# Order of the queries' and shares' pieces, and of the norm's reciprocals, in a hybrid attention layer on one core

## The chip, the core and the metric

The kernel runs on one core of a Trainium2 chip. Time is device microseconds (us) of that core; the time before is the median of three runs. The core has five engines with a stream of instructions each: TensorE (PE, matmuls; PEld are its weight loads), VectorE (DVE), ScalarE (ACT), GpSimd (POOL) and SyncE (SP), which issues most of the transfers (DMAs). Each engine takes its instructions strictly in order, and they wait for one another by semaphores.

## The reference

One layer of an encoder with two attention mixers side by side, over 512 tokens and 16 meta tokens of width 2048. Mixer A has 8 query heads on 2 key heads of 128, with normalised queries and keys and a rotary embedding; mixer B has 8 heads of differential attention: two score maps on halves of 64 columns, the second softmax taken off the first with a factor. Both are gated, joined, projected and normalised.

```python
hn = rmsnorm(h, pre_norm_g[layer])
proj = jnp.einsum('bld,dc->blc', hn, w_in[layer])
qa, ka, va, ga, qb, kb, vb, gb = jnp.split(proj, SPLIT_POINTS, axis=-1)
...
    # mixer A
    s = jnp.einsum('bkgqd,bksd->bkgqs', qs[0], k).astype(jnp.float32) * scale
    p = jax.nn.softmax(s, axis=-1)
    return jnp.einsum('bkgqs,bksd->bkgqd', p.astype(v.dtype), v)
...
    # mixer B
    s1 = jnp.einsum('bhqd,bhkd->bhqk', qs[0], k1).astype(jnp.float32) * scale + bias
    s2 = jnp.einsum('bhqd,bhkd->bhqk', qs[1], k2).astype(jnp.float32) * scale + bias
    a = jax.nn.softmax(s1, axis=-1) - lam * jax.nn.softmax(s2, axis=-1)
    return jnp.einsum('bhqk,bhkd->bhqd', a.astype(v.dtype), v)
...
y = jnp.einsum('blc,cd->bld', jnp.concatenate([ya, yb], axis=-1), w_out[layer])
h = h + rmsnorm(y, post_norm_g[layer])
```

## The kernel before

**Two pieces of each number.** Matmuls run on a rounded type (`fp32r`). Every operand is therefore split into a high piece, rounded by a copy on ACT (`hi`, L349), and a low piece, the rest, by a subtraction on DVE (`lo`, L352); a product takes three matmuls (high·high, low·high, high·low). Weights arrive as `st` and are split into `wh` (ACT, L156) and `wl` (DVE, L157); the list `splits` keeps these instructions, so that others can be put behind them.

**Projections and heads.** The program runs one dense projection after the other (`dense_T`, tile `pd` in PSUM, four banks): for each head of mixer B the gate, values, keys and queries of the next head; then queries, keys and values of mixer A; then mixer A's eight gates; at the end the output product `po`. Between these matmuls PE runs the attention of heads that have begun: scores `sc`, sums of squares `ss`, transpositions `tr` and the products of shares and values `pv`. The class `Lanes` decides the order on PE while the program is written: it keeps a clock of planned matmul time, and each head is a generator that yields the lag (table `LAG`, in us) after which its next matmuls may stand. PE's instructions and the weights' loads keep their program order. The order on the other engines is made by a scheduler from the program, its priorities and its dependences; `tc.issue_after(i)` adds the condition that an instruction stands behind `i`.

**Mixer B.** `queries_B` scales the projection into `qf` (DVE) and makes two maps: `q1`, `q2` (high) and `l1`, `l2` (low), each in two halves of 64 partitions, as keys are stored high and low on the two halves (`s1`, `s2` of `keys_B`). `attention_B` takes four tiles of 128 queries. For each map it computes `sc`, then DVE's reduction L533 puts the bias on, writes `p` and finds the bound `mx`; ACT's exponential (L541) follows, DVE's reciprocal, POOL's normalisation of map 1 (L546), DVE's combination (L548) and two transposes (L460, L462) into `pt`. There is one bank pair for `sc`, so each map's scores wait for the reduction of the last. After two tiles `regroup` sends `pt` to DRAM (`turn`) and back as `pl` by transfers on SP; `p_times_v` splits that into `ph` (ACT) and `pl` (DVE), with `pm` for the meta tokens, and multiplies by the values (`pv`). `finish_B` norms a finished head: squares, `ss` on PE, ACT's square root, four reciprocals of 128 columns (L578, each behind the newest reduction), two multiplications on DVE, and a store of `gB` to `oscr`. `finish_head(h - 1)` is where the program makes sure that this has been written.

**Sums of output weights.** `weigh()` is called five times per head: it issues the load of a block of weights into a scratch tile `ws` on SP, and, one step later, a transfer on POOL's queue that accumulates another block on it (L821).

**Mixer A.** `attention_A` transposes queries, splits them into `qh` and `qlA`, and runs the same steps with one map (reduction L636 to `mxA`, exponential L639, POOL L641). Beside it `silu_A` takes a gate's projection out of PSUM (`gt`, DVE L597) and through ACT's SiLU (L598), and `gate_A` multiplies it on the head's `oA`. ACT loads a table whenever it goes from exponentials to SiLU or back. `half_dead` splits the output of mixer B for the output product (`ah`, `al`, `bh`, `bl`).

## Time and profile before

| | |
|---|---|
| median of three runs | 899.06 us (898.26 to 902.3) |
| the profiled execution, its own time | 901.28 us |
| its span, first to last instruction | 899.5 us |
| mean granted TensorE clock | 0.997 |
| transfers | 185.49 MB, mean 206 GB/s |
| mixer B, 0 to 480 us: PE busy | 469.54 us |
| mixer A, 480 to 743.9 us: PE busy | 253.85 us |
| output product, 743.9 to 899.5 us: PE busy | 146.91 us |

In the profile `L533` is line 533 of the kernel before. A line with a helper (`hi`, `lo`, `mm`) stands for all its callers, so the tile names tell which is meant. A row of a timeline has the start, the duration, engine, line, operation, what it writes and reads, and in brackets the idle time of its engine before it and what ended that. PE's matmuls are pipelined: they start some 0.12 us apart with 264 columns although each is shown as 0.28.

### The profile page before, as it was taken

Reading aid. Unit: us, or ns where it says so; the run is one execution under the profiler, and the core shown is the slowest. Engines: PE = TensorE matmul, PEld = TensorE weight load, DVE = VectorE, ACT = ScalarE, POOL = GpSimd, SP = SyncE. Lnnn points to the kernel's source line nnn. Section 1 sums busy time; section 2 is a strip of 40 time slices with the busy share of each in tenths; the row PEclk is TensorE's granted clock in tenths of the full one; section 3 lists DMA queues with packets and bytes.
Section 4 is the critical chain, followed back from the end, with each engine's and each line's share of the span. In section 5 each row is a group of like instructions: output and inputs, shape, how many; then the busy total and the mean of one; then the engine's idle time right before and its main releaser. Section 6 shows DMA issues by size and latency. Waiting matters only on the chain. (4 is left out here: it accounts for less than half of the span.)

```text
span 899.5 us, 14066 instructions
## 1 busy us (share of the span) xinstructions
PE 870.3 (97%) x5130; PEld 769.9 (86%) x5130; DVE 631.4 (70%) x1137; ACT 497.9 (55%) x844; POOL 124.9 (14%) x168
## 2 busy tenths in 40 slices
PE   9999999999999999999999999999999989999996
PEld 8999898998989889888898888987878778888884
DVE  6577786857857568485683485788666675886886
ACT  6565564637546474464654444656566555665561
POOL 0100220211011121101120021342111210000010
PEclk9999999999999999999999999999999999999998
DMA  9754979887696877868553334456566658989883
GB/s 336 262 163 144 236 216 258 201 233 194 198 260 155 247 212 222 241 170 238 143 181 94 105 94 149 144 168 182 170 181 217 181 167 283 317 275 308 272 276 152
DMA packets 80677, 185.49 MB, mean 206 GB/s; under 512 B 15136, under 2 KB 38560, under 8 KB 80224
## 3 DMA queue, kind: packets, MB, share of 16 engines
q1 hardware_dynamic: 75856, 167.81, 57.1%
q0 software_dynamic: 4608, 16.78, 11.3%
q8 instruction: 40, 0.66, 0.3%
q14 instruction: 29, 0.24, 0.1%
q10 hardware_dynamic: 144, 0.01, 0.0%
HBM read 158.34 MB, written 59.77 MB: 242 GB/s over the span
## 5 line engine op out<-in xcount | busy, mean ns | idle before, releaser
L61 PE MATMUL pd<-xh,wh 128*128 128x264 f32 (+1 forms) x992 | 325.8, 328 | 0.0
L61 PE MATMUL pd<-xl,wh 128*128 128x264 f32 (+1 forms) x992 | 323.1, 326 | 0.0
L61 PE MATMUL pd<-xh,wl 128*128 128x264 f32 (+1 forms) x992 | 322.7, 325 | 0.4 <-DVE wl L157 0.4
L156 ACT ACTIVATE wh<-st 128x1024 fp32r<-128x1024 f32 (+2 forms) x159 | 165.5, 1041 | 187.1 <-PE pd L61 92.4
L157 DVE TENSOR_TENSOR wl<-st,wh 128x1024 fp32r<-128x1024 f32 (+2 forms) x159 | 191.1, 1202 | 86.6 <-ACT wh L156 86.2
L61 PEld LDWEIGHTS pd<-xh,wl 128*128 128x128 f32 x992 | 186.5, 188 | 16.5 <-DVE wl L157 0.8
L61 PEld LDWEIGHTS pd<-xh,wh 128*128 128x128 f32 x992 | 186.8, 188 | 12.3 <-ACT wh L156 0.2
L61 PEld LDWEIGHTS pd<-xl,wh 128*128 128x128 f32 x992 | 187.0, 189 | 10.6
L541 ACT ACTIVATE p<-p,mx 128x528 f32<-128x528 f32 x64 | 47.1, 736 | 58.8 <-DVE mx L533 58.6
L61 PE MATMUL pd<-wh,xh 128*128 128x512 f32 x128 | 50.4, 394 | 0.0
L460 DVE STREAM_TRANSPOSE pt<-p 128x512 f32<-128x512 f32 x64 | 45.0, 702 | 7.1 <-POOL p L641 6.4
L61 PE MATMUL pd<-wh,xl 128*128 128x512 f32 x128 | 49.9, 390 | 0.0
L61 PE MATMUL pd<-wl,xh 128*128 128x512 f32 x128 | 49.9, 390 | 0.0
L639 ACT ACTIVATE p<-p,mxA 128x528 f32<-128x528 f32 x32 | 23.6, 737 | 46.2 <-DVE mxA L636 46.1
L533 DVE CUSTOM_DVE_ANT_0 p<-sc,dist 128x528 f32<-128x528 f32 x64 | 43.9, 686 | 4.7 <-PE sc L61 4.3
L821 POOL DMA_DIRECT2D ws<-in_w_o_dram x32 | 26.7, 834 | 146.0 <-DMA ws<-ws 64.0
L546 POOL TENSOR_SCALAR p<-p,sm 128x528 f32<-128x528 f32 x32 | 22.8, 711 | 173.2 <-DVE sm L543 164.9
L641 POOL TENSOR_SCALAR p<-p,smA 128x528 f32<-128x528 f32 x32 | 26.4, 826 | 119.1 <-DVE smA L640 97.9
L352 DVE TENSOR_TENSOR pl<-pl,ph 128x1024 fp32r<-128x1024 f32 x32 | 39.2, 1226 | 3.2 <-ACT ph L349 2.3
L61 PE MATMUL pv<-pl,vh 128*128 128x256 f32 x128 | 36.6, 286 | 4.4 <-DVE pl L352 4.4
L61 PE MATMUL sc<-s,q 128*128 128x264 f32 x128 | 35.3, 295 | 3.9 <-DVE mx L533 3.9
L548 DVE SCALAR_TENSOR_TENSOR p<-p,c 128x528 f32<-128x528 f32 x32 | 24.5, 766 | 20.7 <-POOL p L546 20.5
(223 smaller groups left out, 1569.8 us busy)
## 6 DMA issues: line engine op xcount, KB each, us to landing
st<-in_w_t_dram SPq DMA_DIRECT2D x82, 512.0 KB, 5.1
turn<-pt SPq DMA_DIRECT2D x32, 544.0 KB, 3.0
pl<-turn SPq DMA_DIRECT2D x128, 128.0 KB, 3.9
ws<-in_w_o_dram POOLq DMA_DIRECT2D x32, 512.0 KB, 8.1
st<-ws SPq DMA_DIRECT2D x32, 512.0 KB, 4.4
st<-in_w_o_dram SPq DMA_DIRECT2D x22, 512.0 KB, 4.3
ws<-in_w_o_dram SPq DMA_DIRECT2D x16, 512.0 KB, 6.7
ws<-ws SPq DMA_DIRECT2D x16, 512.0 KB, 7.0
```

The costliest lines, as they stand in the source:

```text
L61: self._add(self.nc.tensor.matmul(out, lhsT, rhs, start=start, stop=stop, **kw), us)
L156: splits.append((nc.scalar.activation(wh[:, c], st[:, c], AF.Copy), nc.vector.tensor_tensor(out=wl[:, c], in0=st[:, c], in1=wh[:, c].bitca ...
L157: nc.vector.tensor_tensor(out=wl[:, c], in0=st[:, c], in1=wh[:, c].bitcast(F32), op=ALU.subtract)))
L352: nc.vector.tensor_tensor(out=dst, in0=src, in1=h.bitcast(F32), op=ALU.subtract)
L460: nc.vector.transpose(pt[:, :1024].rearrange("p (m c t q) -> p c m t q", m=4, c=TT, t=2)[:, :, :, j], p[:, NM:].rearrange("p (c m q) -> p ...
L533: maxima.append(nc.vector.tensor_tensor_reduce(out=two(p), in0=sc[:, :, :HALF], in1=two(dist[:, w0:w0 + NT]), scale=-0.125 / slope(h), sca ...
L541: nc.scalar.activation(p2[m], p2[m], AF.Exp, scale=-1.0, bias=mx[:, m:m + 1], accum_out=sm[:, m:m + 1])
L546: nc.gpsimd.tensor_scalar(out=p2[0], in0=p2[0], scalar1=sm[:, 0:1], scalar2=1.0, op0=ALU.mult, op1=ALU.mult)
L548: nc.vector.scalar_tensor_tensor(out=p2[0], in0=p2[1], scalar=c2, in1=p2[0], op0=ALU.mult, op1=ALU.add)
L639: nc.scalar.activation(p, p, AF.Exp, scale=-1.0, bias=mx, accum_out=sm)
L641: nc.gpsimd.tensor_scalar(out=p, in0=p, scalar1=sm, scalar2=1.0, op0=ALU.mult, op1=ALU.mult)
L821: nc.gpsimd.dma_start(out=dst, in_=src, accum_op=ALU.add)
```

## The change

It changes orders and no arithmetic.

- `queries_B` and `keys_B` write their pieces map by map: both high pieces of map 1, its two low ones, then map 2.
- `q_last` holds the newest queries' last high and last low piece, and `p_last` the shares' `pm` and `pl`; `behind_all` puts instructions behind these. In `p_times_v`, `ph` and `pm` stand behind the queries' last high piece, `pl` behind their last low one.
- Gates (`silu_A`) and the splits of `half_dead` stand behind the newest `pm` and `pl`; exponentials of mixer A behind the newest `pm`.
- `finish_B` yields after each of the first three reciprocals, where it yielded after the second alone, so that each next one goes behind a later reduction.
- `finish_head(h - 1)` is called after the keys' projection; in its old place the program only makes sure that the head's scores and last product are written (`products_B`).

```diff
--- before.py
+++ after.py
@@ -346,10 +346,10 @@
     L, U = slice(0, 64), slice(64, 128)
 
     def hi(dst, src):
-        nc.scalar.activation(dst, src, AF.Copy)
+        return nc.scalar.activation(dst, src, AF.Copy)
 
     def lo(dst, src, h):
-        nc.vector.tensor_tensor(out=dst, in0=src, in1=h.bitcast(F32), op=ALU.subtract)
+        return nc.vector.tensor_tensor(out=dst, in0=src, in1=h.bitcast(F32), op=ALU.subtract)
 
     def keys_B(pss, after=nullcontext):
         kf = ap.tile([P, NT], F32, name="kf", tag="tT")
@@ -357,10 +357,9 @@
         s1 = ap.tile([P, NT], F32R, name="s1", tag="s1")
         s2 = ap.tile([P, NT], F32R, name="s2", tag="s2")
         with after():
-            hi(s1[L], kf[L])
-            hi(s2[U], kf[U])
-            lo(s1[U], kf[L], s1[L])
-            lo(s2[L], kf[U], s2[U])
+            for s, a, b in ((s1, L, U), (s2, U, L)):
+                hi(s[a], kf[a])
+                lo(s[b], kf[a], s[a])
         return s1, s2
 
 
@@ -383,6 +382,17 @@
 
     def slope(h):
         return 2.0 ** (h - 2)
+
+
+    q_last, p_last = [None, None], [None, None]
+
+    @contextmanager
+    def behind_all(*ins):
+        with ExitStack() as stack:
+            for i in ins:
+                if i is not None:
+                    stack.enter_context(tc.issue_after(i))
+            yield
 
     def queries_B(h, pss, after=nullcontext):
         qf = ap.tile([P, NT], F32, name="qf", tag="tT")
@@ -395,14 +405,12 @@
         l2 = ap.tile([P, SEQ], F32R, name="l2", tag="ql", bufs=4)
         to, qf = [dealt(t) for t in (q1, l1, q2, l2)], by_token(qf)
         with after():
-            hi(to[0][L], qf[L])
-            hi(to[2][U], qf[U])
-            hi(to[0][U], qf[L])
-            hi(to[2][L], qf[U])
-            lo(to[1][L], qf[L], to[0][L])
-            lo(to[3][U], qf[U], to[2][U])
-            lo(to[1][U], qf[L], to[0][L])
-            lo(to[3][L], qf[U], to[2][U])
+
+            for q, l, a, b in (to[:2] + [L, U], to[2:] + [U, L]):
+                hi(q[a], qf[a])
+                q_last[0] = hi(q[b], qf[a]).ins
+                lo(l[a], qf[a], q[a])
+                q_last[1] = lo(l[b], qf[a], q[a]).ins
         return (q1, l1), (q2, l2)
 
     def values(pss, lag=LAG["vals"]):
@@ -483,10 +491,11 @@
         pm = ap.tile([96, 2 * P], F32R, name="pm", tag="pm", bufs=1)
         pt = pl.bitcast(F32)
 
-        with tc.issue_after(splits[-1][0].ins):
+        with behind_all(splits[-1][0].ins, q_last[0]):
             hi(ph, pt)
-            hi(pm[0:32], pf)
-        lo(pl, pt, ph)
+            p_last[0] = hi(pm[0:32], pf).ins
+        with behind_all(q_last[1]):
+            p_last[1] = lo(pl, pt, ph).ins
         nc.gpsimd.tensor_scalar(out=pm[32:64], in0=pm[0:32].bitcast(F32), scalar1=1.0,
                                 scalar2=1.0, op0=ALU.mult, op1=ALU.mult)
         lo(pm[64:96], pf, pm[0:32])
@@ -555,6 +564,7 @@
                             LAG["pB"])
             if half == 0:
                 yield LAG["scB"]
+        products_B[h] = last
         over[h] = lanes.spawn(finish_B(h, o), LAG["fin"], last)
 
     def finish_B(h, o):
@@ -576,7 +586,7 @@
 
             with tc.issue_after(maxima[-1].ins):
                 nc.vector.reciprocal(out=sq[:, tq], in_=sq[:, tq])
-            if t == 1:
+            if t < TT - 1:
                 yield LAG["scB"]
         nc.vector.tensor_tensor(out=o, in0=o, in1=sq, op=ALU.mult)
         nc.vector.scalar_tensor_tensor(out=gB[h], in0=o, scalar=sgc, in1=gB[h],
@@ -594,8 +604,9 @@
 
     def silu_A(pss):
         g = gp.tile([P, SEQ], F32, name="gt", tag="gt")
-        nc.vector.tensor_tensor(out=g, in0=pss[0], in1=rB[:, NM:], op=ALU.mult)
-        nc.scalar.activation(g, g, AF.Silu)
+        with behind_all(*p_last):
+            nc.vector.tensor_tensor(out=g, in0=pss[0], in1=rB[:, NM:], op=ALU.mult)
+            nc.scalar.activation(g, g, AF.Silu)
         return g
 
     def gate_A(h, g):
@@ -614,8 +625,8 @@
         tr = ptr.tile([P, 512], F32, name="tr", tag="tr")
         for t in range(TT):
             transpose(tr[:, t * P:(t + 1) * P], qn[t][:, h % 4, :], ident)
-        hi(dealt(qh), by_token(tr))
-        lo(dealt(ql), by_token(tr), dealt(qh))
+        q_last[0] = hi(dealt(qh), by_token(tr)).ins
+        q_last[1] = lo(dealt(ql), by_token(tr), dealt(qh)).ins
         yield LAG["qA"]
         while not k_task[3]:
             yield 0.3
@@ -636,7 +647,8 @@
                 maxima.append(nc.vector.tensor_tensor_reduce(
                     out=two(p), in0=sc[:, :, :HALF], in1=two(zed[0][:, :NT]), scale=-ASCALE,
                     scalar=3.0e38, op0=ALU.add, op1=ALU.min, accum_out=mx))
-                nc.scalar.activation(p, p, AF.Exp, scale=-1.0, bias=mx, accum_out=sm)
+                with behind_all(p_last[0]):
+                    nc.scalar.activation(p, p, AF.Exp, scale=-1.0, bias=mx, accum_out=sm)
                 nc.vector.reciprocal(out=sm, in_=sm)
                 nc.gpsimd.tensor_scalar(out=p, in0=p, scalar1=sm, scalar2=1.0,
                                         op0=ALU.mult, op1=ALU.mult)
@@ -872,7 +884,7 @@
     v = values(pss)
     with behind():
         gB = [gate(first[2], "gB0")] + [None] * (NH - 1)
-    heads, over = [None] * (2 * NH), [None] * (2 * NH)
+    heads, over, products_B = [None] * (2 * NH), [None] * (2 * NH), [None] * NH
 
     def finish_head(h):
         lanes.finish(heads[h])
@@ -890,11 +902,14 @@
             pss = dense_T(KEYS)
             if h:
                 weigh()
-                finish_head(h - 1)
+
+                lanes.finish(heads[h - 1])
+                lanes.finish(products_B[h - 1])
             v = values(pss)
             ks = keys_B(dense_T(KEYS))
             if h:
                 weigh()
+                finish_head(h - 1)
             qs = queries_B(h + 1, dense_T(REAL))
     weigh()
     def start_heads(grp, qn, q_task, k, v):
@@ -957,7 +972,8 @@
                     with tc.issue_after(splits[-4][1].ins):
                         TTv(out=sd, in0=st, in1=sd, op=SUB)
                     st = sd
-                split(to[i], st)
+                with behind_all(*p_last):
+                    split(to[i], st)
 
     for h in range(NH):
         if h == 5:
```

**DVE, head 4's queries.** These are DVE's instructions around the queries of mixer B's head 4. Rows name line, operation, output, inputs and shape; line numbers of the change are its own, so L542 is the reduction that was L533. Before:

```order
L390 SCALAR_TENSOR_TENSOR qf_2948<-pd_2865,rB_537 128x512
L157 TENSOR_TENSOR wl_2966<-st_2870,wh_2965 128x1024
L352 TENSOR_TENSOR pl_2761<-pl_2761,ph_2983 128x1024
L352 TENSOR_TENSOR l1_2952<-qf_2948,q1_2950 64x4x4x32
L352 TENSOR_TENSOR l2_2953<-qf_2948,q2_2951 64x4x4x32
L352 TENSOR_TENSOR l1_2952<-qf_2948,q1_2950 64x4x4x32
L352 TENSOR_TENSOR l2_2953<-qf_2948,q2_2951 64x4x4x32
L352 TENSOR_TENSOR pm_2984<-pt_2614,pm_2984 32x256
L533 ISA p_3005,mx_2998<-sc_3000,dist_558 128x528
```

and with the change:

```order
L400 SCALAR_TENSOR_TENSOR qf_2948<-pd_2872,rB_537 128x512
L157 TENSOR_TENSOR wl_2966<-st_2877,wh_2965 128x1024
L352 TENSOR_TENSOR l1_2952<-qf_2948,q1_2950 64x4x4x32 x2
L352 TENSOR_TENSOR l2_2953<-qf_2948,q2_2951 64x4x4x32 x2
L352 TENSOR_TENSOR pl_2749<-pl_2749,ph_2977 128x1024
L352 TENSOR_TENSOR pm_2978<-pt_2595,pm_2978 32x256
L542 ISA p_3005,mx_2998<-sc_3000,dist_558 128x528
```

The low part `pl` of the shares moved from in front of the four `l` to behind them, and the two pieces of `l1` now stand together in front of those of `l2`.

**DVE, the reciprocals of head 3's norm**, during the scores of head 4 (L533, in the change L542, is a score reduction; L578, in the change L588, a reciprocal). Before:

```order
L533 ISA p_3187,mx_3180<-sc_3182,dist_558 128x528
L533 ISA mx_3180 128x1
L460 STREAM_TRANSPOSE pt_2997<-p_3086 128x4x4x32
L462 STREAM_TRANSPOSE pt_2997<-p_3086 128x32
L578 RECIPROCAL sq_3073<-sq_3073 128x128 x4
L533 ISA p_3229,mx_3180<-sc_3224,dist_558 128x528
L533 ISA mx_3180 128x1
L581 TENSOR_TENSOR oB_2419<-oB_2419,sq_3073 128x512
L157 TENSOR_TENSOR wl_3193<-st_3017,wh_3192 128x1024
L582 SCALAR_TENSOR_TENSOR gB3_2514<-oB_2419,sgc_551,gB3_2514 128x512
L543 RECIPROCAL sm_3181<-sm_3181 128x2
L533 ISA p_3271,mx_3264<-sc_3266,dist_558 128x528
```

and with the change:

```order
L542 ISA p_3180,mx_3173<-sc_3175,dist_558 128x528
L542 ISA mx_3173 128x1
L468 STREAM_TRANSPOSE pt_2997<-p_3083 128x4x4x32
L470 STREAM_TRANSPOSE pt_2997<-p_3083 128x32
L588 RECIPROCAL sq_3070<-sq_3070 128x128 x2
L542 ISA p_3218,mx_3173<-sc_3213,dist_558 128x528
L542 ISA mx_3173 128x1
L588 RECIPROCAL sq_3070<-sq_3070 128x128
L157 TENSOR_TENSOR wl_3192<-st_3017,wh_3191 128x1024
L552 RECIPROCAL sm_3174<-sm_3174 128x2
L554 TENSOR_TENSOR c2_3223<-sm_3174,nlam_557 128x1
L542 ISA p_3261,mx_3254<-sc_3256,dist_558 128x528
```

Of the four in a row two are left in front of the reduction `mx_3180` (now `mx_3173`), one stands behind it, and the fourth follows behind the next reduction, further on. The multiplications L581 and L582 come later still.

**DVE, around the queries `qlA_7274` of mixer A** (L597, in the change L608, takes a gate out of PSUM; L460 and L462, in the change L468 and L470, are transposes of shares). Before:

```order
L157 TENSOR_TENSOR wl_7265<-st_7105,wh_7264 128x1024
L352 TENSOR_TENSOR pl_7032<-pl_7032,ph_7218 128x1024
L352 TENSOR_TENSOR pm_7219<-pt_6958,pm_7219 32x256
L640 RECIPROCAL smA_7235<-smA_7235 128x1
L352 TENSOR_TENSOR qlA_7274<-tr_7275,qh_7273 128x4x4x32
L460 STREAM_TRANSPOSE pt_7184<-p_7194 128x4x4x32
L462 STREAM_TRANSPOSE pt_7184<-p_7194 128x32
```

and with the change:

```order
L157 TENSOR_TENSOR wl_7265<-st_7105,wh_7264 128x1024
L352 TENSOR_TENSOR pl_7032<-pl_7032,ph_7218 128x1024
L352 TENSOR_TENSOR pm_7219<-pt_6958,pm_7219 32x256
L652 RECIPROCAL smA_7235<-smA_7235 128x1
L608 TENSOR_TENSOR gt_7258<-pd_6931,rB_537 128x512
L468 STREAM_TRANSPOSE pt_7184<-p_7194 128x4x4x32
L470 STREAM_TRANSPOSE pt_7184<-p_7194 128x32
L468 STREAM_TRANSPOSE pt_7184<-p_7243 128x4x4x32
L470 STREAM_TRANSPOSE pt_7184<-p_7243 128x32
L352 TENSOR_TENSOR qlA_7274<-tr_7275,qh_7273 128x4x4x32
```

The gate product `gt_7258`, which stood further ahead, and both pairs of transposes moved in front of `qlA_7274`.

**POOL, mixer B's head 4** (L821, in the change L833, is the accumulating transfer; L546, in the change L555, the normalisation of a tile's shares). Before:

```order
L490 TENSOR_SCALAR pm_2984<-pm_2984 32x256
L821 DMA ws100_580<-in_w_o_dram 128x1024
L821 DMA ws101_581<-in_w_o_dram 128x1024
L546 TENSOR_SCALAR p_3005<-p_3005,sm_2999 128x528
L546 TENSOR_SCALAR p_3086<-p_3086,sm_3080 128x528
L546 TENSOR_SCALAR p_3187<-p_3187,sm_3181 128x528
L546 TENSOR_SCALAR p_3271<-p_3271,sm_3265 128x528
L821 DMA ws102_582<-in_w_o_dram 128x1024
```

and with the change:

```order
L499 TENSOR_SCALAR pm_2978<-pm_2978 32x256
L833 DMA ws100_580<-in_w_o_dram 128x1024
L833 DMA ws101_581<-in_w_o_dram 128x1024
L555 TENSOR_SCALAR p_3005<-p_3005,sm_2999 128x528
L555 TENSOR_SCALAR p_3083<-p_3083,sm_3077 128x528
L833 DMA ws102_582<-in_w_o_dram 128x1024
L555 TENSOR_SCALAR p_3180<-p_3180,sm_3174 128x528
L555 TENSOR_SCALAR p_3261<-p_3261,sm_3255 128x528
```

The two transfers ahead of the first normalisation keep their place, and the transfer to `ws102` moved from behind the fourth to between the second and the third.

## The prediction

> **What bounds the kernel now.** I read the page's busy shares first, then the chain that ended last, then the list of what TensorE (PE) waits for, then timelines around those waits.
>
> ```profile
> PE 870.3 (97%) x5130; PEld 769.9 (86%) x5130; DVE 631.4 (70%) x1137; ACT 497.9 (55%) x844; POOL 124.9 (14%) x168
> PE po L61 16%; PE pd L61 1%; PE pv L61 1%; DVE y L1151 0%; DMA pt<-turn 0%; ACT jko L1066 0%; DVE y L1069 0%; DVE y L1157 0%; DVE pl L352 0%; DVEq L1259 0%; ACT bh L349 0%; DVE bl L352 0%; DVE ssy L1162 0%; ACTq L1066 0%
> ```
>
> PE is busy for 97% of the span; the change leaves its 5130 matmuls as they are. The last 16% of the span, the output product `po`, is one chain on PE, where the change touches nothing. So the time can change only by what PE waits in the attention before it.
>
> ```profile
> PE sc L61 <- DVE l L352: 4.7, 4, 1.2
> PE pv L61 <- DVE pl L352: 4.4, 4, 1.5
> PE sc L61 <- DVE mx L533: 3.9, 7, 0.9
> PE sc L61 <- DVE qlA L352: 2.1, 4, 1.1
> PE sc L61 <- ACT qh L349: 1.1, 1, 1.1
> PE pv L61 <- ACT ph L349: 0.9, 2, 0.5
> ```
>
> This is the list of PE's waits, grouped by what ended them: us in total, times, the longest. These six rows add to 17.1 us, 1.9% of the span: that is nearly all there is to win. Against it stand the waits that the change makes itself. A difference of 0.5%, 4.5 us, is about what a measurement of this kernel can tell from no change.
>
> **Part 1, the share's low part behind the queries' (mixer B).** In head 4 VectorE (DVE) makes the low part `pl` of the last head's shares, then the four low parts `l` of the new queries:
>
> ```profile
> 258.57 1.22 DVE L352 TENSOR_TENSOR pl<-pl,ph 128x1024 fp32r<-128x1024 f32 x1
> 259.71 2.88 DVE L352 TENSOR_TENSOR l<-qf,q 64x512 fp32r<-64x512 f32 x4
> 261.84 0.39 PE L61 MATMUL sc<-s,l 128*128 128x264 f32 x1 [1.17 <-DVE l L352]
> 262.07 0.28 PE L61 MATMUL sc<-s,q 128*128 128x264 f32 x1
> ```
>
> The first score product waits 1.17 us for map 1's second piece, the third of the four. The change takes `pl` (1.22 us) from in front, and makes map 1's second piece the second, 0.7 us (2.88/4) sooner. Head 3 shows the new order already, since there the scheduler had put `pl` last:
>
> ```profile
> 204.20 2.81 DVE L352 TENSOR_TENSOR l<-qf,q 64x512 fp32r<-64x512 f32 x4
> 206.34 0.39 PE L61 MATMUL sc<-s,l 128*128 128x264 f32 x1
> 207.03 1.23 DVE L352 TENSOR_TENSOR pl<-pl,ph 128x1024 fp32r<-128x1024 f32 x1
> ```
>
> There no wait is listed; only the matmul's 0.39 in place of 0.28 tells that it came out of a short stop. I leave 0.2 us in each of heads 4 to 7: 4.7 − 4 × 0.2 = **−3.9 us**. What then comes late is `pl` itself, by the `l`s' 2.9 us; no `pv` of mixer B has a row that waits on it now (all four are in mixer A). If that cover is gone, it costs at most 2.9 us a head.
>
> **Part 2, one reciprocal per score.** In head 4 the four reciprocals of head 3's norm stand as a block in front of a score reduction `mx`:
>
> ```profile
> 282.03 3.34 DVE L578 RECIPROCAL sq<-sq 128x128 f32<-128x128 f32 x4
> 286.00 0.39 PE L61 MATMUL sc<-s,q 128*128 128x264 f32 x1 [0.68 <-DVE mx L533]
> ...
> 384.27 0.39 PE L61 MATMUL sc<-s,q 128*128 128x264 f32 x1 [0.29 <-DVE mx L533]
> 392.60 0.39 PE L61 MATMUL sc<-s,q 128*128 128x264 f32 x1 [0.43 <-DVE mx L533]
> ```
>
> With two in front and one behind each of the next reductions, `mx` starts 1.7 us earlier and the wait of 0.68 goes. Of the seven waits on `mx` five stand behind such reciprocals; I keep the two others, 0.29 and 0.43 in head 6: 3.9 − 0.7 = **−3.2 us**. The finish of a head (two multiplications on DVE, the store of `gB` on SP's queue) comes later, but nobody reads it before the output. On SP a load of the weights' sums, `ws`, moves in front of `turn<-pt`, and a weight load `st` behind it; on POOL one accumulating transfer moves from after a head's four normalisations to between the second and the third. I cost both at nothing, since transfers to `turn` and loads have slack (no `pv` waits here, one `pd` wait of 0.4 in all); if the slack is not there, 0.9 us of issue for one `ws` load in each of heads 2 to 7, 5 us.
>
> **Part 3, what takes the place of these waits.** POOL's first normalisation of a head stands in order behind two accumulating transfers that wait for loads:
>
> ```profile
> 265.79 0.84 POOL L821 DMA_DIRECT2D ws<-in_w_o_dram  x1 [3.74 <-DMA ws<-in_w_o_dram]
> 270.05 0.81 POOL L821 DMA_DIRECT2D ws<-in_w_o_dram  x1 [3.42 <-DMA ws<-in_w_o_dram]
> 270.94 0.71 POOL L546 TENSOR_SCALAR p<-p,sm 128x528 f32<-128x528 f32 x1
> ...
> 271.69 0.77 DVE L548 SCALAR_TENSOR_TENSOR p<-p,c 128x528 f32<-128x528 f32 x1 [3.84 <-POOL p L546]
> 273.36 0.64 DVE L533 CUSTOM_DVE_ANT_0 p<-sc,dist 128x528 f32<-128x528 f32 x1
> 274.06 0.39 PE L61 MATMUL sc<-s,q 128*128 128x264 f32 x1
> 324.84 0.77 DVE L548 SCALAR_TENSOR_TENSOR p<-p,c 128x528 f32<-128x528 f32 x1 [1.16 <-POOL p L546]
> 381.89 0.77 DVE L548 SCALAR_TENSOR_TENSOR p<-p,c 128x528 f32<-128x528 f32 x1 [3.33 <-POOL p L546]
> ```
>
> DVE sits idle for 3.84 us until POOL's `p` is there, and the next reduction, at 273.36, stands behind it. Its scores' bank is wanted by PE for the next scores at 274.06: just in time, because PE had lost 1.17 us before. These rows are set by transfers, not by PE. If PE comes 1.0 us sooner (1.17 − 0.2), and by the new order 0.7 us sooner still, it waits there: 1.7 us in head 4. Head 6 has the same gap (3.33) and already waits behind it for 0.29; it loses its 1.0 us again. Heads 5 and 7 I cost at nothing; at most 1.7 us each. Sum **+2.7 us**.
>
> **Part 4, mixer A.** Here a gate's product and table load, and exponentials, move behind the shares' parts.
>
> ```profile
> 627.61 0.39 PE L61 MATMUL sc<-kh,qh 128*128 128x264 f32 x1 [1.09 <-ACT qh L349]
> ...
> 713.09 1.75 SPq L473 DMA_DIRECT2D pl<-turn  x4
> 717.36 1.04 ACT L349 ACTIVATE ph<-pl 128x1024 fp32r<-128x1024 f32 x1
> 718.55 0.69 DVE L597 TENSOR_TENSOR gt<-pd,rB 128x512 f32<-128x512 f32 x1 [0.91 <-PE pd L61]
> 719.16 1.22 DVE L352 TENSOR_TENSOR pl<-pl,ph 128x1024 fp32r<-128x1024 f32 x1
> 720.43 0.39 PE L61 MATMUL pv<-pl,vh 128*128 128x256 f32 x1 [1.48 <-DVE pl L352]
> ...
> 728.86 1.04 ACT L349 ACTIVATE ph<-pl 128x1024 fp32r<-128x1024 f32 x1
> 731.89 0.39 PE L61 MATMUL pv<-pl,vh 128*128 128x256 f32 x1 [1.43 <-DVE pl L352]
> ```
>
> At 627.61 ScalarE's `qh` was late behind an exponential's table load; that load now comes behind, −1.1. At 720.43 the gate's 0.69 us (0.61 from start to start) stands between `ph` and `pl`; without it, and with `ph` ahead of the exponential, I take −0.9 of 1.48: the rest is bounded by the transfers, issued at 713.09 and read at 717.36. The last product (731.89, and 0.4 on `ph` just before) has its `ph` 11 us after those of the product before, behind the halves `al` and `bl`; those now stand behind it: −1.9. The other waits on `pl` (4.4 − 1.48 − 1.43 = 1.5) and the longer one on `ph` (0.5) are near their transfers' arrival: of 2.0 I take −0.8. Together −4.7. Against it:
>
> ```profile
> 673.26 0.67 DVE L352 TENSOR_TENSOR qlA<-tr,qh 128x512 fp32r<-128x512 f32 x1
> 673.85 0.70 DVE L460 STREAM_TRANSPOSE pt<-p 128x512 f32<-128x512 f32 x1
> ...
> 673.99 0.39 PE L61 MATMUL sc<-kh,qlA 128*128 128x264 f32 x1 [1.05 <-DVE qlA L352]
> ```
>
> The new order puts a gate (0.69 as at 718.55), this transpose and a second like it, with their tails some 0.75 each, in front of `qlA`: 0.61 + 2 × 0.75 = 2.1 more on a wait of 1.05. Part 4: **−2.6 us**. Its gates run about one projection later; their PSUM banks are wanted four projections later.
>
> **The sum.** −3.9 − 3.2 + 2.7 − 2.6 = −7.0. A first matmul after a wait lasts 0.39 where the next has 0.28, so each of some 13 waits fewer (four on `l`, five on `mx`, one on `qh`, four of the six on shares, less the new one in head 4) adds 0.11: −1.4. In all **−8.4 us** against the profiled execution's 901.28 (span 899.5 and 1.8 outside it): 892.9. That run lies 2.2 over the median of the three shown, 899.06, from which the sum gives 890.7. I put **891.5**.
>
> **The rivals.**
> 1. *Transfers keep it all in mixer B.* Each of heads 4 to 7 loses 1.7 at POOL's first normalisation: 6.8 for 2.7, so −4.3, 896.0 with the same shift as above. For it: the idle rows of 3.84 and 3.33. Against it: in head 5 the same row has a gap of only 1.16 (at 324.84).
> 2. *Gates and transposes ahead of `qlA`.* If what I see once happens in all four heads that wait there, 3 × 2.1 more: 897.8. For it: 2.1 us are waited on `qlA` already. Against it: the order shows it in one place.
> 3. *The work is only named anew.* DVE is 70% busy; PE then waits for the next thing in its line, and no wait gets shorter: 899. For it: three engines' orders move, no work goes. Against it: head 3.
> 4. *Slower: POOL and DVE meet.* `pl` now stands where POOL normalises:
>
> ```profile
> 584.58 2.21 POOL L641 TENSOR_SCALAR p<-p,smA 128x528 f32<-128x528 f32 x1 [3.28 <-DVE smA L640]
> 585.08 1.23 DVE L352 TENSOR_TENSOR pl<-pl,ph 128x1024 fp32r<-128x1024 f32 x1
> ```
>
> POOL's 0.71 us (at 270.94) became 2.21 beside `pl`, 1.5 more, and the transposes, the transfers and `pv` stand behind it. If it falls on PE in all eight heads of mixer A, 12.0 us, and part 4's 4.7 don't come: −8.4 + 4.7 + 12.0 = +8.3, 908. It decides from six heads on. Against it: it shows at few places now, with `pl` in each head. The Trainium skill's page "SBUF — State Buffer" (section "SBUF: two separate sides") says that a DVE operation with two SBUF inputs and a POOL operation shut each other out for a whole instruction. By that rule each meeting costs the whole of the other, as in this row, and the trace agrees (2.21 against 0.71); by shared bandwidth it would be less.
> 5. *All waits go:* −17.1 and 0.11 for each of 22: 880.
>
> **Chances.** Forecast 0.50; rivals in order 0.15, 0.16, 0.08, 0.07, 0.04. Its own range is 887 to 894.5. The range reaches from 885.5 to 898.5, which takes in rivals 1 and 2 and leaves out 3, 4 and 5. Faster by over 0.5% (under 894.6): the forecast nearly whole, rival 5 and a part of 1, 0.64. Within 0.5%: 0.28. Slower: 0.08.
>
> **What would show it.** The row of `sc` on `l` gone or under 1 us in all; reciprocals in pairs and singles, and the row on `mx` not gone but moved to the reduction behind POOL's `p` in heads 4 and 6; the last `pv` without a wait; `qlA` at about 4 us. The prediction is wrong if `pv` waits on `pl` in mixer B, if the idle time before POOL's `p` shrinks with PE coming earlier, or if `pd` begins to wait for `wl`.

## The result and the profile after

| | before | with the change |
|---|---|---|
| median | 898.97 us (898.26 to 902.3, 4 runs) | 888.81 us (886.89 to 889.98, 4 runs) |
| ratio | | 0.9875, 95% interval 0.9845 to 0.9906 |
| profiled execution, its time | 901.28 us | 888.59 us |
| its span | 899.5 us | 886.8 us |

The change made the kernel 1.25% faster; the forecast was 891.5 us, with a range of 885.5 to 898.5. The page's shares of the kernel with the change, and the list of PE's waits (us in total, times, the longest):

```profile
PE 868.8 (98%) x5130; PEld 772.7 (87%) x5130; DVE 631.0 (71%) x1137; ACT 497.6 (56%) x843; POOL 126.7 (14%) x168
PE sc L61 <- DVE qlA L352: 3.9, 3, 3.0
PE sc L61 <- DVE mx L542: 2.4, 6, 0.4
PE sc L61 <- DVE mxA L647: 1.5, 1, 1.5
...
```

The work is the same; PE's busy time fell a little, from 870.3 to 868.8 us. Of the six rows of the forecast those on `l`, `pl`, `qh` and `ph` are gone. Two are left: `qlA`, now longer, and `mx`, which is a new wait under an old name. The waits named in the two lists fell from 20.3 to 9.2 us in all, by 11.1. The span fell by 12.7. There are 14 waits fewer, and at 0.11 us for each slow first matmul after a wait that is the other 1.6 us. That the two add to 12.7 is in part chance, as the granted clock differs between the two traces (under Mixer A below). (Of e3 and e5 further down one disturbed run each, of 1748.59 and 1227.35 us, is left out.)

**Head 4's queries.** DVE's timeline of the kernel with the change, and PE's row behind it:

```profile
257.51 2.79 DVE L352 TENSOR_TENSOR l<-qf,q 64x512 fp32r<-64x512 f32 x4
260.34 1.43 DVE L352 TENSOR_TENSOR pl<-pl,ph 128x1024 fp32r<-128x1024 f32 x1
261.80 0.42 DVE L352 TENSOR_TENSOR pm<-pt,pm 32x256 fp32r<-32x256 f32 x1
262.25 0.71 DVE L542 CUSTOM_DVE_ANT_0 p<-sc,dist 128x528 f32<-128x528 f32 x1
...
263.11 0.36 PE L61 MATMUL sc<-s,q 128*128 128x264 f32 x1 [0.39 <-DVE mx L542]
```

The four `l` come straight behind `qf` and the weights' `wl`, and no score waits for them. But `pl` and `pm` (1.43 and 0.42 us) now stand in front of the head's *first score reduction*, and the second map's scores wait for that one: 0.39 us here, and about 0.4 in each of heads 2 to 7. These six are all that the row on `mx` holds now.

**Head 3's reciprocals**, on the same timeline further on:

```profile
279.66 1.72 DVE L588 RECIPROCAL sq<-sq 128x128 f32<-128x128 f32 x2
281.30 0.65 DVE L542 CUSTOM_DVE_ANT_0 p<-sc,dist 128x528 f32<-128x528 f32 x1
...
281.87 0.95 DVE L588 RECIPROCAL sq<-sq 128x128 f32<-128x128 f32 x1
```

Two, then a reduction, then one: no score waits behind them. POOL's first normalisation of the head and DVE's combination that waits for it:

```profile
266.82 0.82 POOL L833 DMA_DIRECT2D ws<-in_w_o_dram  x1 [0.58 <-DMA ws<-in_w_o_dram]
267.72 0.71 POOL L555 TENSOR_SCALAR p<-p,sm 128x528 f32<-128x528 f32 x1
...
268.47 0.77 DVE L557 SCALAR_TENSOR_TENSOR p<-p,c 128x528 f32<-128x528 f32 x1 [2.48 <-POOL p L555]
```

The second accumulating transfer was issued at 266.82 where it had been 270.05, so POOL's `p` came 3.2 us sooner (the head itself 1.1 us: its `l` came 2.2 sooner, of which 1.1 is `pl`), and DVE's idle time before the combination shrank from 3.84 to 2.48. No wait of PE stands behind it.

**Mixer A.** DVE and PE around the `qlA` of the forecast, and ACT and DVE at the product that had waited 1.43 us at 731.89:

```profile
663.25 0.67 DVE L608 TENSOR_TENSOR gt<-pd,rB 128x512 f32<-128x512 f32 x1
...
665.24 0.65 DVE L352 TENSOR_TENSOR qlA<-tr,qh 128x512 fp32r<-128x512 f32 x1
...
665.95 0.48 PE L61 MATMUL sc<-kh,qlA 128*128 128x264 f32 x1 [3.02 <-DVE qlA L352]
...
714.40 1.04 ACT L349 ACTIVATE ph<-pl 128x1024 fp32r<-128x1024 f32 x1
715.67 1.22 DVE L352 TENSOR_TENSOR pl<-pl,ph 128x1024 fp32r<-128x1024 f32 x1
```

The gate and the transposes stand in front of `qlA`, and PE waits 3.02 us for it, 2.0 more than before. `ph` and `pl` of that last product stand in front of the halves' splits, at 714.40 and 715.67 where `ph` was at 728.86, and no `pv` is on the list of waits.

Behind that long wait PE runs at half clock for a while. Its rows there, and just after:

```profile
666.88 0.63 PE L61 MATMUL pd<-xh,wh 128*128 128x512 f32 x1
667.31 0.63 PE L61 MATMUL pd<-xl,wh 128*128 128x512 f32 x1
...
669.72 0.40 PE L61 MATMUL pd<-xl,wh 128*128 128x512 f32 x1
669.95 0.39 PE L61 MATMUL pd<-xh,wl 128*128 128x512 f32 x1
```

The same matmuls start 0.43 us apart instead of 0.23; the granted clock is 0.50 from 666.2 to 669.4, and once more from 598 to 601. In the trace of before it is 1.00 all through mixer A, from 480 to 740 us. By the spacing of the starts each stretch costs some 1.6 us (an estimate), 3.2 together, and the matmuls count as busy meanwhile. As PE's busy time fell by 1.5 us all the same, some 3 us of gain must lie outside the list, most likely in stops too short for it.

The stretch at 666 goes with the wait of 3.0 us: of the five traces with that wait (this one, e3, a0, e14, e17) all but e3's have a granted clock under 1 between 655 and 680 us, and none of the nine with a wait of 1.0 to 1.1 on `qlA` there. What decides it in e3 is not known. The stretch near 600 comes in kernels of all kinds (e1 and e7 have it too).

### The profile page after: what moved, and what is told of

Its sections match the earlier page's. It is cut to its first block, busy times and chain, and to the rows that moved or that the text cites. A ratio compares the mean times of both kernels' runs of the same rounds, so it can differ in the third digit from the quotient of the medians.

```text
span 886.8 us, 14070 instructions
## 1 busy us (share of the span) xinstructions
PE 868.8 (98%) x5130; PEld 772.7 (87%) x5130; DVE 631.0 (71%) x1137; ACT 497.6 (56%) x843; POOL 126.7 (14%) x168
## 3 DMA queue, kind: packets, MB, share of 16 engines
q0 software_dynamic: 4608, 16.78, 11.1%
## 5 line engine op out<-in xcount | busy, mean ns | idle before, releaser
L468 DVE STREAM_TRANSPOSE pt<-p 128x512 f32<-128x512 f32 x64 | 44.8, 699 | 8.2 <-POOL p L653 7.7
L555 POOL TENSOR_SCALAR p<-p,sm 128x528 f32<-128x528 f32 x32 | 22.7, 708 | 168.2 <-DVE sm L552 167.9
L542 DVE CUSTOM_DVE_ANT_0 p<-sc,dist 128x528 f32<-128x528 f32 x64 | 44.2, 690 | 3.5 <-PE sc L61 2.6
L833 POOL DMA_DIRECT2D ws<-in_w_o_dram x32 | 26.8, 837 | 117.9 <-DMA ws<-in_w_o_dram 53.3
L499 POOL TENSOR_SCALAR pm<-pm 32x256 fp32r<-32x256 f32 x32 | 23.0, 719 | 116.3 <-ACT pm L349 80.4
L647 DVE CUSTOM_DVE_ANT_0 p<-sc,zed 128x528 f32<-128x528 f32 x32 | 22.3, 698 | 21.9 <-PE sc L61 21.7
```

Source lines behind the costliest of these rows:

```text
L468: nc.vector.transpose(pt[:, :1024].rearrange("p (m c t q) -> p c m t q", m=4, c=TT, t=2)[:, :, :, j], p[:, NM:].rearrange("p (c m q) -> p ...
L499: nc.gpsimd.tensor_scalar(out=pm[32:64], in0=pm[0:32].bitcast(F32), scalar1=1.0, scalar2=1.0, op0=ALU.mult, op1=ALU.mult)
L542: maxima.append(nc.vector.tensor_tensor_reduce(out=two(p), in0=sc[:, :, :HALF], in1=two(dist[:, w0:w0 + NT]), scale=-0.125 / slope(h), sca ...
L555: nc.gpsimd.tensor_scalar(out=p2[0], in0=p2[0], scalar1=sm[:, 0:1], scalar2=1.0, op0=ALU.mult, op1=ALU.mult)
L833: nc.gpsimd.dma_start(out=dst, in_=src, accum_op=ALU.add)
```

## The experiments

Times are medians; ratios are to runs of the kernel before on the same chip in the same hours. Its medians there were 900.05 us for e1, e2, e3 and e6, 899.58 for a0, e5, e9 and e11, and 900.63 for e7, e14, e16 and e17.

### The three parts, one at a time

**e1**: of the diff only `queries_B` map by map, `q_last` (in mixer A too) and, in `p_times_v`,

```diff
-        with tc.issue_after(splits[-1][0].ins):
+        with behind_all(splits[-1][0].ins, q_last[0]):
             hi(ph, pt)
             hi(pm[0:32], pf)
-        lo(pl, pt, ph)
+        with behind_all(q_last[1]):
+            lo(pl, pt, ph)
```

> Only the queries' pieces map by map, with the shares' parts behind them; gates, exponentials, reciprocals and the finish of a head as before. Theory (each part moves its own waits): the row of sc on l (4.7 us) is gone; the shares' pl now stands in front of each head's first score reduction, so a new wait of 0.4 us on mx shows in heads 2 to 7 (2.4 us) beside the old 3.9 on mx; mixer A as before (pl 4.4, qlA 2.1). Span 2 to 3 us shorter than before. Rival (POOL's first normalisation, timed by its two transfers, gives the gain back in heads 4 and 6): waits on mx of 1.7 and 1.0 us more at the reduction behind that normalisation, span within 0.5 us of before.

897.99 us, ratio 0.9984 (0.9967 to 1.0001). The waits' row, and DVE and PE behind POOL's first normalisation in head 4:

```profile
PE sc L61 <- DVE mx L541: 5.1, 11, 0.7
...
271.16 0.77 DVE L556 SCALAR_TENSOR_TENSOR p<-p,c 128x528 f32<-128x528 f32 x1 [4.54 <-POOL p L554]
...
273.54 0.39 PE L61 MATMUL sc<-s,q 128*128 128x264 f32 x1 [0.73 <-DVE mx L541]
```

The row on `l` is gone, and the waits of 0.4 on `mx` are there in heads 4 to 7 (0.16 in head 3). Both were expected, the second from head 2 on. But the rival's wait is there too: in head 4 PE comes earlier and waits 0.73 us for the reduction behind POOL's `p`. By the medians the queries' part alone keeps about 2 of its 4.7 us, and its interval just takes in no change. (The 1.1 us on `qh` in mixer A are gone here as well.)

**e2**: of the diff only the yields of `finish_B` and the later `finish_head(h - 1)`, with `products_B`.

> Only the reciprocals one per score and the later finish of a head; queries, shares, gates and exponentials as before. Theory: sc on l stays at 4.7 us; the waits on mx of heads 2 to 7 behind reciprocals (0.51, 0.21, 0.68, 0.90, 0.87) go, so the row on mx falls from 3.9 to 0.7 us; mixer A as before. Span 3 to 4 us shorter. Rival (the moved loads and accumulating transfers of the weights' sums hold POOL's third normalisation or a weight load): a new row on mx behind that normalisation, or pd on wl, of 1 us or more, and a span less than 2 us shorter.

898.03 us, ratio 0.9978 (0.9963 to 0.9993).

```profile
PE sc L61 <- DVE l L352: 7.0, 6, 1.2
```

The row on `mx` has gone altogether, more than expected; but `l` now has six waits for four, since the scheduler has put `pl` in front of the `l`s in heads 2 and 3 as well. The expectation that `l` stays was wrong, and the time fell by 2.0 us where 3 to 4 were expected. POOL's first normalisation is not late in this trace: in heads 3 to 7 DVE's combination waits 0.72 to 0.93 us for it, little more than the product's own 0.71, where before it was 0.98 to 3.84. So this run does not show what the block of reciprocals costs by itself. No `pd` waits, so the moved loads hold nothing.

**e3**: of the diff only what stands behind `p_last`: `silu_A`, the exponentials of mixer A, and the splits of `half_dead`.

> Only gates, halves' splits and mixer A's exponentials behind the shares' parts; the rest as before. Theory: everything that mixer A gained comes from this: pv on pl (4.4) and on ph (0.9) gone, sc on qh from 1.1 to 0.2, sc on qlA from 2.1 to 3.9 with one wait of 3.0; mixer B as before (l 4.7, mx 3.9). Span 5 to 6 us shorter. Rival (mixer A's shares need the queries' order of part 1 too): pv on pl keeps 1.5 us or more, span under 4 us shorter.

894.26 us (889.66 to 897.6), ratio 0.9934 (0.9911 to 0.9958). The trace is of the shortest of these executions:

```profile
PE sc L61 <- DVE qlA L352: 3.9, 3, 3.0
...
PE sc L61 <- DVE mx L543: 1.1, 3, 0.5
```

Mixer A is as in the full change: nothing on `pl`, `ph` and `qh`, and 3.0 us on `qlA`. The whole gain there comes from this part. The second row was not expected. DVE's order in mixer B is that of the kernel before, and yet `mx` has 1.1 us where the trace of before had 3.9. So those waits are no property of the order alone, and executions of one kernel differ in them: here DVE's combination in heads 4 and 6 waits 1.52 and 1.03 us for POOL's `p`, where it was 3.84 and 3.33. The granted clock differs too: from 0.992 to 0.997 over these eight executions, the shortest at 0.997 and the longest at 0.993, and this trace has no stretch at half clock before the output product.

By ratios the three parts give 0.16, 0.22 and 0.66%, 1.04% together, where the full change gives 1.25%, well within their intervals. The new order of the keys' pieces (`keys_B`) is in none of the three, and was not tried by itself.

### What the waits on the reduction are

**e7**: the kernel before, without the accumulating transfers, so that the sums of the output weights lack their second term.

```diff
-            nc.gpsimd.dma_start(out=dst, in_=src, accum_op=ALU.add)
+            pass
```

> The kernel before, with the accumulating transfers on POOL's queue left out, so that the sums of the output weights lack their second term. Theory A (the old waits on mx are the four reciprocals in front of the reduction): the row on mx stays at 3 us or more, l at 4.7, time within 1.5 us of before. Theory B (the old waits on mx come about because POOL's first normalisation is late behind its transfers and everything of the head slides into the reciprocals): the row on mx falls under 1 us, l stays, time 3 to 5 us under before.

896.09 us, ratio 0.9955 (0.9942 to 0.9969).

```profile
PE sc L61 <- DVE l L352: 4.7, 4, 1.2
...
PE sc L61 <- DVE mx L533: 0.7, 2, 0.5
...
280.00 3.34 DVE L578 RECIPROCAL sq<-sq 128x128 f32<-128x128 f32 x4
283.26 0.65 DVE L533 CUSTOM_DVE_ANT_0 p<-sc,dist 128x528 f32<-128x528 f32 x1
```

Theory B: five of the seven old waits on `mx` go when POOL's transfers go, although the block of four reciprocals still stands in front of the same reductions (at 280.00 in head 4). DVE's combination now waits 0.72 us in heads 3 to 7. When `p` is late it pushes everything of the head behind it, and then the block meets a reduction that PE needs; both are needed for these waits. Only the first two (0.51 and 0.21, heads 2 and 3) are there without a late `p`. One trace alone would not carry this, since e3's had lost waits on `mx` with the transfers in place; but the time, 4.5 us under before, is clear of the noise. The 1.1 us on `qh` are gone here too.

**e17**: the changed kernel, with the same edit.

> The changed kernel with the accumulating transfers left out, so that the sums of the output weights lack their second term. Theory (its waits on mx come from pl and pm in front of the first reduction, not from transfers): the six waits of 0.4 us stay, 2.4 in all, qlA at 3.0; time 0 to 2 us under the changed kernel. Rival (transfers are behind these as well): the row on mx is gone and the time is 3 us or more under it.

889.09 us, ratio 0.9868 (0.985 to 0.9887).

```profile
PE sc L61 <- DVE mx L542: 2.4, 6, 0.4
```

The six waits stay as they are, and the time is that of the changed kernel. With the change POOL's transfers cost nothing that these runs could tell, and these waits are the shares' pieces in front of the first reduction.

**e14**: the changed kernel without the second part, `if t == 1` in `finish_B` and `finish_head(h - 1)` in its old place.

> The changed kernel without its second part: reciprocals and the finish of a head as before. Theory (the parts add): waits on mx of 5 us as with the queries alone (0.4 in each head and 0.6 to 0.7 behind reciprocals in heads 2, 4, 5, 6), mixer A as in the changed kernel; time 2 to 3 us over the changed kernel. Rival (the second part does nothing that the first has not done): within 1 us of the changed kernel.

889.28 us, ratio 0.99 (0.9866 to 0.9933); but of the six runs four lie at 887.74 to 889.35 and two at 896.29 and 897.15. The trace is of the 896.29:

```profile
PE sc L61 <- DVE mx L542: 7.9, 15, 0.9
...
336.34 3.35 DVE L588 RECIPROCAL sq<-sq 128x128 f32<-128x128 f32 x4
...
340.31 0.39 PE L61 MATMUL sc<-s,q 128*128 128x264 f32 x1 [0.87 <-DVE mx L542]
```

Here the block of four costs 0.87 us in head 5, and 0.69 to 0.90 at the same place in heads 4, 6 and 7. POOL's `p` is late in this trace: DVE's combination waits 4.67, 4.34, 3.00, 2.78 and 3.29 us for it in heads 3 to 7 (0.99, 2.48, 0.72, 1.29 and 0.98 in the trace of the change). The granted clock is not the reason: its mean is 0.994 here and 0.993 there. So neither the theory nor the rival holds for all runs: by their times, leaving the second part out cost four of them nothing and two of them some 8 us. Ten runs of the changed kernel show none above 891.42. That the second part removes the slower group is thus likely, with ten runs against six, but not proven.

### What could still be had

**a0**: the changed kernel again.

> The changed kernel once more, on the chip of the next three, as their reference. All theories: six waits of 0.4 us on mx, one of 3.0 on qlA, none on l, pl, ph; time 10 to 11 us under before.

888.73 us, ratio 0.9875 (0.9852 to 0.9899), with the same waits, one more of 0.29 on `mx`, and 0.6 at the start of the kernel.

**e5**:

```diff
-        q_last[1] = lo(dealt(ql), by_token(tr), dealt(qh)).ins
+        with tc.high_priority(300):
+            q_last[1] = lo(dealt(ql), by_token(tr), dealt(qh)).ins
```

> The changed kernel with one thing moved: mixer A's low query piece qlA comes ahead of the gate's product and the transposes. Theory (the loss of 2 us on qlA is the gate and the transposes in front of it, and nothing behind them is late): qlA's wait falls from 3.0 to 1.0, no new wait, time 2 us under the changed kernel. Rival (the transposes then are late for the shares' transfers): pv waits on pl or ph by 1 us or more, time within 1 us of the changed kernel.

884.64 us, ratio 0.9827 (0.98 to 0.9854). Two rows of the list of waits:

```profile
PE sc L61 <- DVE mx L542: 2.4, 6, 0.4
PE sc L61 <- DVE qlA L352: 1.9, 3, 1.1
```

The 2.0 us are won, and no `pv` waits. The median is 4.1 us under a0's, twice that: this trace has no stretch at half clock before the output product, and those of a0 and of the change each have one of some 1.6 us behind the wait of 3.0. So the long wait probably cost more than its length.

**e6**: as e5, and each head's first reduction with `tc.high_priority(300)`, which puts it in front of `pm`'s low part.

> The changed kernel with two subtractions' neighbours reordered: each head's first score reduction of mixer B comes ahead of pm's low part, and mixer A's qlA comes ahead of the gate and the transposes. Theory (what is left is order on VectorE): the six waits of 0.4 on mx fall under 0.1 each (2.4 to under 0.5 us), qlA's 3.0 falls to about 1.0, so the span is 4 to 5 us shorter than the changed kernel's 886.8. Rival (the scores are held by the shares' pl itself or by the transposition's bank): the waits of 0.4 stay or move to the next reduction, span within 2.5 us of the changed kernel's.

882.97 us, ratio 0.9814 (0.9791 to 0.9837). DVE and PE in head 3:

```profile
215.70 0.77 DVE L558 SCALAR_TENSOR_TENSOR p<-p,c 128x528 f32<-128x528 f32 x1 [3.25 <-POOL p L556]
...
217.97 0.39 PE L61 MATMUL sc<-s,q 128*128 128x264 f32 x1 [0.55 <-DVE mx L543]
```

The six waits of 0.4 have gone, and as many others have come, 3.1 us in all: this one and 0.73 in head 6 behind POOL's `p`, and four of 0.42 to 0.48 elsewhere. That the 0.4 us had hidden POOL's lateness is not shown by this: the transfers were later themselves here, and the combination in head 3 came at 215.70, where in the trace of the change it came at 213.17.

**e9**: as e5, with `pl` and `pm` of mixer B written 3.0 us of planned time later, behind the newest reduction.

```diff
-        with behind_all(q_last[1]):
+        if ab == "B":
+            yield 3.0
+        with behind_all(q_last[1], maxima[-1].ins):
             p_last[1] = lo(pl, pt, ph).ins
...
-        lo(pm[64:96], pf, pm[0:32])
-        yield LAG["pv" + ab]
+        with behind_all(maxima[-1].ins):
+            lo(pm[64:96], pf, pm[0:32])
+        yield LAG["pv" + ab] - (3.0 if ab == "B" else 0.0)
```

> As the last, and in mixer B the low parts pl and pm stand behind each head's first score reduction, by being written 3 us of planned time later. Theory (the 0.4 us on mx is pl and pm in front of it, and PE then runs into POOL's first normalisation, which waits for its two transfers): the six waits of 0.4 go, waits of 0.5 to 0.8 on mx come back at the reduction behind POOL's first normalisation in one to three heads, time 3 to 5 us under the changed kernel. Rival (nothing else holds the scores): no row on mx above 0.5 us in all, time 5 to 6 us under the changed kernel.

884.45 us, ratio 0.9821 (0.9794 to 0.9848).

```profile
PE sc L61 <- DVE mx L545: 1.7, 4, 0.5
```

The six waits went and four came: 0.31 behind POOL's first `p` in head 4, and three of 0.47 to 0.48 in heads 3, 4 and 6, one tile later. Against e5 that is no difference that its interval could tell.

**e11**: e9 without the accumulating transfers (the edit of e7).

> As the last, with the accumulating transfers on POOL's queue left out, so that the sums of the output weights lack their second term. Theory (POOL's transfers hold the first normalisation): POOL's p of each head comes as soon as its reciprocal, the row on mx falls under 0.5 us, time 1 to 4 us under the kernel with them. Rival (the reductions themselves set the pace): the waits on mx stay, time within 1 us of it.

879.56 us, ratio 0.9771 (0.9747 to 0.9796). There is no row on `mx` any more. POOL's first normalisation of head 4:

```profile
264.41 0.71 POOL L558 TENSOR_SCALAR p<-p,sm 128x528 f32<-128x528 f32 x1 [5.30 <-DVE sm L555]
```

It now waits for its reciprocal `sm`, and comes 3.7 us before that of e9 (268.06). The waits of e9 were POOL's transfers. The gain, 4.9 us between the medians, is more than the 1.7 of the listed waits (with 0.11 each, 2.1). Between the two traces PE's idle time fell by 2.2 us and its busy time by 2.1; both have one stretch at half clock near 600 us, so that is not the reason, and where the rest comes from was not tried.

**e16**: e9 with a head's first normalisation on ScalarE, a kernel that computes everything.

```diff
+                if t == 0:
+                    nc.scalar.activation(p2[0], p2[0], AF.Copy, scale=sm[:, 0:1])
+                else:
...
```

> The kernel with qlA first and the shares behind the reduction, and in mixer B the first of a head's four normalisations on ScalarE in place of POOL: the same product, off the queue with the transfers. Theory (POOL's transfers hold that normalisation): DVE's combination no longer waits 2 to 3 us for it in any head, the row on mx falls under 0.6 us, time 2 to 4 us under the kernel with all four on POOL (884). Rival (ScalarE is late itself by 0.7 us a head, in front of the weights' high parts): pd waits on wh or wl, or sc on mx as much as now; time within 1 us or over it.

880.58 us, ratio 0.9775 (0.9759 to 0.9791): faster than both kernels, 8 us under the change. ACT and DVE in head 4:

```profile
265.05 0.74 ACT L559 ACTIVATE p<-p,sm 128x528 f32<-128x528 f32 x1 [0.23 <-DVE sm L555]
...
265.82 0.77 DVE L563 SCALAR_TENSOR_TENSOR p<-p,c 128x528 f32<-128x528 f32 x1 [0.61 <-ACT p L559]
```

The combination waits 0.61 us for its share where it waited 2.87 in e9; the row on `mx` is gone with the transfers still in place, and no new wait above 0.4 us has come.

## Why the prediction was right, and where it was not

The forecast's direction and most of its mechanisms held; that the total came so near is partly luck, since errors of opposite sign met in it. The sum was −8.4 us against −12.7 between the profiled executions, and −10.2 between medians. Term by term, in listed waits:

| step | predicted | measured |
|---|---|---|
| part 1, `l` | −3.9 | −4.7, and +2.4 new on the first reduction |
| part 2, old waits on `mx` | −3.2 | −3.9 |
| part 3, POOL's first `p` | +2.7 | 0 |
| part 4, mixer A | −2.6 | −4.5 |
| start-up after a wait | −1.4 | −1.6 |

A wait of 0.4 at the start of the kernel, on `wl`, is in the trace of before and not in that of the change, and makes up the rest. The 2.7 that did not come and the 2.4 that were not expected cancel. Not in the sum at all are the granted clock, some 3.2 us against the change, and some 3 us of short stops that went.

- **Part 1** was right on `l`: head 3's row told the new order truly, and nothing was left of the 0.2 us. It was wrong on what comes late. It looked for that at the `pv` products, where `pl` is used, and not at the next instruction of DVE's queue. Head 3 had the clue: a first reduction behind `pl` and `pm`.
- **Part 2** had the size nearly right and half of the cause. It laid the waits to the block of reciprocals in front; e7 shows that the block stays and five of the seven waits go when POOL's transfers go. The reciprocals were where the lateness came out: with a late `p` the block costs up to 0.90 us a head (e14).
- **Part 3** failed in its place. The mechanism is real: e1 has it in head 4 with 0.73 us, e6 and e9 have it, e11 and e16 remove it. In the changed kernel it shows nowhere. PE loses 0.4 us just before, at the first reduction, which may hide some of it. And the row at 270.05, taken as fixed, was not: the transfer came 3.2 us sooner, some 2 of them beyond the head's own lead. The prediction named the shrinking of DVE's idle time as a sign that this step is wrong, and it did shrink (3.84 to 2.48). What made the load land sooner was not tried for itself. With the second part alone (e2) DVE waits at most 0.93 us for `p` in heads 3 to 7, and without it (e1, e14) up to 4.67; but e6 and e9, which have that part, wait up to 3.41 again.
- **Part 4**: `qlA` came out as worked out, 3.0 against 1.05 + 2.1. The sizes that were off are those of the shares' products: 2.0 us at 661, 707 and 708 were taken to be bounded by transfers, with only 0.8 of them to be had, and 0.9 of 1.48 at 720; all went. The 1.1 on `qh` were gone in e1 and e7 as well, where the gates and exponentials stand as before, so they need not be this part's. The last product's `ph` had stood on ACT behind `bh`, not behind `al` and `bl`. And the forecast counted the wait on `qlA` alone, not the half clock that follows it in most traces.
- **The rivals.** The first (transfers keep it all in mixer B) is what e1 and e6 show in part, but not the change. The second (gates ahead of `qlA`) stayed at the one place. Of the third (only names change) the row on `mx` is a small piece, 2.4 us. For the fourth (POOL and DVE meet), POOL's `p` in mixer A still has one instruction of 2.21 us and a median of 0.71; it did not spread. (The row of 2.21 at 584.58 overlaps another product of DVE, on `qn` from 584.44, and not `pl` alone.)

## What to carry to other kernels

When an instruction is moved back in an engine's queue, look at what now stands right behind it in that queue before looking at who reads its result. A wait that disappears lets its engine run into the next late thing, so a list of waits is worked off one at a time, and each removal is to be followed by a new list. A wait's releaser is only the last link: to learn who set the pace, take away the suspected cause further back (here a queue of transfers) and see which waits stay.

## What was not expected of the hardware

An engine that is 14% busy held up PE, which is 97% busy: in POOL's queue a 0.71 us product stood behind transfers that waited up to 5.8 us for loads (in e6). A wait of 3.0 us of PE went with a stretch at half clock right behind it in four of five traces; in the trace of the change that cost some 1.6 us on top of the wait (an estimate).

Executions of one kernel differ: e3 and e14 spread over 8 to 9 us with an unchanged order. Two things change with them, and the runs don't separate them: how late POOL's `p` comes (in head 4 DVE waits 3.84 us for it in the trace of before, 1.52 in e3's, with the same order), and the granted clock (e7's longest run, 897.8 us, had 0.994, its four shortest, up to 896.26, 0.997 or 0.998). A single profiled execution, then, says which waits can occur, but not that each one does in every run.
